# First heads and values split on VectorE, x ahead of the weights, gate operands ahead of the second norm, four banks in a turn

## The chip, the core and the metric

The kernel runs on one core of a Trainium2 chip. The metric is the device time of one execution in microseconds (us), the median of three runs. A core has five engines that each work through a queue of their own in order: TensorE (PE, matrix products), VectorE (DVE), ScalarE (ACT), GpSimd (POOL) and SyncE (SP), which here issues the transfers from the chip's memory (HBM) into SBUF. PE writes to PSUM, which has eight banks. An instruction that waits for another engine holds up what stands behind it in its own queue.

## The reference

Two layers of an encoder over 512 rows of width 1024. Layer 0 mixes rows with a gated linear recurrence (8 heads, both directions), layer 1 with latent attention (16 heads). Around both stand norms, a squared-ReLU MLP and a gated input per layer:

```python
for i in range(DEPTH):
    h = rms_norm(x, pre_mix[i])
    h = hgrn2_mixer(h, ...) if i == 0 else mla_mixer(h, positions, ...)
    x = x + rms_norm(h, post_mix[i])
    h = rms_norm(x, pre_mlp[i])
    h = jnp.square(jax.nn.relu(h @ w1[i])) @ w2[i]
    x = x + rms_norm(h, post_mlp[i])
    e = (p[i] @ w_ple_proj[i]) * jax.nn.sigmoid(x @ w_ple_gate[i])
    x = x + rms_norm(e, ple[i])
```

The mixers' inner loops are left out; no formula changes.

## The kernel before

**Tiling.** The 512 rows are four tiles of 128 rows. The first two tiles are called `a`, the last two `b`. Every product is made in three passes of split operands: an operand is rounded to a high part (`whi`, `ah`) and the remainder is the low part (`wlo`, `al`); PE then does high·high, low·high and high·low with 512 columns (256 where only one half of the rows is ready).

**Weights.** The class `Weights` (`W`) keeps a plan: transfers into buffers `raw` (two of them, `raw_bufs=2`), and pieces of 128x1024 called jobs. For each job ACT rounds `whi` (L109) and the job's engine subtracts to get `wlo`. That engine is `VN` (VectorE, written in a fixed order with its neighbours) unless the job names another one: `nc.vector` (VectorE, but free to be placed elsewhere in its queue) or `nc.gpsimd` (POOL; then in two halves, L112). `W.hold(keys)` splits up to four jobs ahead of what is used (`ahead=4`) and hands out the pieces; five pairs live at once (`split_bufs=5`). A `raw` buffer is free, and the next transfer is issued by SP, when the last job on it is split. Pieces are numbered in the plan's order.

**Queue order.** The program is written once; a scheduler sorts it into the queues. Where `keep(True)` is on, PE and `VN` instructions stay in the order of the source.

**The start.** `x0` to `x3` are loaded, tile 0 is normed (`normed((0,))`), then tile 1, then 2 and 3 together. The sum of squares is made by ACT for even tiles and by VectorE's `bn_stats` for odd ones; a chain of small VectorE instructions (`rq_i`, `rq_m`, `rq_n`, `rq_t`, `rx`) makes the reciprocal root. `first_values` multiplies with the four first value operands, numbers 0 to 3, which POOL splits. POOL also makes the rope tables.

**Mixer to MLP.** `mixer_to_mlp` multiplies the mixer's output with its gain row (`row("post_mix", l)`, loaded at the function's beginning, L837), adds the residual, norms, and turns.

**Turns.** `turned` turns a normed tile pair with PE (128x128 transposes against `ident`) into banks, from which ACT and VectorE split `ah` and `al`. There are three kinds of banks: `mm` (five), `sm` (two), `nm` (one). A turn uses four banks, one for each quarter of the width; with `sm` for all four the third quarter waits until the first has been read.

**MLP to gate.** In `mlp_to_gate` the last MLP products (`last`) of tiles `a` are made, then `chain(a)` norms them (`F` and `H`), `last` for `b`, `turned(a)`, `chain(b)`, then `W.hold` for the gate's operands 132 to 135, `gate` for `a`, `turned(b)`, `gate` for `b`. Layer 1 does the same with later numbers. Then comes the code that leads to the attention: `chain`, `turned` into the operands of `min` (145 and 146 are its last pieces).

**Attention's first part.** `query_latent`, `rope`, and per pair of heads `plan_heads`' three jobs (`uqn` 128x768, `uqr` 128x384, `ukv` 128x1024), all split by POOL; POOL also adds the rope terms (`rope_d`, L1291) and makes the remainders `stk` (L1367). The norms of the query and of the key/value latents are chains of small VectorE instructions (`nv`, `rq_...`, `nr`).

## Time and profile before

| | us |
|---|---|
| median of three runs | 1586.87 (1586.75 to 1590.89) |
| profiled execution | 1591.48 |
| its span on the core | 1589.8 |
| PE busy in it | 1529.7 (96 %) |
| VectorE, ACT, POOL busy | 1018.7, 772.3, 214.7 |

Three things are read from the trace: where PE stood idle and which engine ended that wait; in which stretches the granted clock of PE was half; and what the engine that ended the wait had been doing until then. In the rows, a bracket at the end gives the idle time just before an instruction and what released it; "x4" means four instructions in one row, whose time is that of the four together.

### The profile page before, as it was taken

To read this page: it belongs to the slowest core of one execution; us is meant where nothing else is said; L and a number is where in the kernel's file an instruction comes from. 1 tells how busy PE (TensorE), PEld (TensorE's weight loads), DVE (VectorE), ACT (ScalarE), POOL (GpSimd) and SP (SyncE) were. 2 spreads that over 40 slices of the span, in tenths; PEclk is the share of its full clock that TensorE was granted. 3 is DMA by queue.
4 is the path that set the end of the run, shared out by engine and by line. 5 is a ranking of instruction groups with operands and counts; after the bars stand their busy time and mean duration, and the time that the engine had idled before them with its cause. 6 is when DMAs were issued, how large, how long until landed. Compare 5 with 4: busy or idle time off the path is not lost.

```text
span 1589.8 us, 19297 instructions
## 1 busy us (share of the span) xinstructions
PE 1529.7 (96%) x7379; PEld 1265.5 (80%) x7379; DVE 1018.7 (64%) x1832; ACT 772.3 (49%) x1317; POOL 214.7 (14%) x232
## 2 busy tenths in 40 slices
PE   7999999998999999998898999999999999999987
PEld 6888888878888787876787888888788887878866
DVE  6678568653674949455757774378464748576365
ACT  4554455254654444433544654366355645454332
POOL 7133132200000000000125322342000000000000
PEclk8999999999999999999999999999999999999999
DMA  5622222145242322313411110211452140604211
GB/s 161 175 64 80 80 80 80 40 139 190 83 147 66 130 82 79 107 53 107 140 58 42 56 53 28 80 58 54 162 196 80 50 162 1 212 1 159 80 53 53
DMA packets 109951, 147.87 MB, mean 93 GB/s; under 512 B 4781, under 2 KB 78114, under 8 KB 109602
## 3 DMA queue, kind: packets, MB, share of 16 engines
q1 hardware_dynamic: 109282, 145.58, 28.1%
q8 instruction: 58, 0.95, 0.3%
q10 hardware_dynamic: 576, 1.05, 0.2%
q14 instruction: 35, 0.29, 0.1%
HBM read 138.23 MB, written 8.39 MB: 92 GB/s over the span
## 4 chain that ended last, share of the span: by engine, by line
PE 86%; DVE 8%; ACT 3%; issue 1%; DMA 1%; POOL 0%; SPq 0%; DVEq 0%; ACTq 0%; POOLq 0%
PE mm L147 80%; PE sm L147 5%; DVE wlo L147 1%; PE nm L147 1%; ACT whi L109 1%; DVE rq_t L147 1%; DMA x<-in_x 1%; DVE al L341 0%; DVE rope_d L1288 0%; DVE rope_d L1289 0%; DVE al L343 0%; DMA row<-in_gains 0%; ACT ah L342 0%; DVE ol L341 0%; ACT junk L855 0%
## 5 line engine op out<-in xcount | busy, mean ns | idle before, releaser
L147 PE MATMUL mm<-ah,whi 128*128 128x512 f32 (+1 forms) x912 | 333.9, 371 | 1.9 <-ACT e L996 0.9
L147 PE MATMUL mm<-ah,wlo 128*128 128x512 f32 (+1 forms) x912 | 330.9, 370 | 4.8 <-DVE wlo L147 4.8
L147 PE MATMUL mm<-al,whi 128*128 128x512 f32 (+1 forms) x912 | 319.2, 370 | 0.0
L109 ACT CAST whi<-raw 128x1024 fp32r<-128x1024 f32 (+3 forms) x195 | 196.8, 1016 | 251.8 <-PE mm L147 196.1
L147 DVE TENSOR_TENSOR wlo<-raw,whi 128x1024 fp32r<-128x1024 f32 x161 | 202.0, 1266 | 159.2 <-ACT whi L109 158.7
L147 PEld LDWEIGHTS mm<-ah,wlo 128*128 128x128 f32 x912 | 172.7, 189 | 32.5 <-DVE wlo L147 5.0
L147 PEld LDWEIGHTS mm<-ah,whi 128*128 128x128 f32 x912 | 172.7, 189 | 32.1 <-ACT whi L109 2.6
L147 PEld LDWEIGHTS mm<-al,whi 128*128 128x128 f32 x912 | 164.9, 190 | 28.2 <-DVE al L343 0.9
L147 PE MATMUL mm<-wlo,oh 128*128 128x512 f32 x400 | 159.3, 398 | 3.3 <-DVE wlo L147 3.3
L147 PE MATMUL mm<-whi,ol 128*128 128x512 f32 x400 | 157.7, 397 | 0.0
L147 PE MATMUL mm<-whi,oh 128*128 128x512 f32 x400 | 154.7, 400 | 2.8 <-DVE F L1039 2.8
L147 DVE TENSOR_TENSOR wlo<-r,whi 128x1024 fp32r<-128x1024 f32 x84 | 102.1, 1221 | 75.6 <-ACT whi L109 75.6
L109 ACT CAST whi<-r 128x1024 fp32r<-128x1024 f32 x84 | 87.1, 1049 | 86.9 <-PE mm L147 86.9
L147 PE MATMUL mm<-wlo,ah 128*128 128x512 f32 x304 | 120.5, 396 | 8.6 <-DVE wlo L147 8.6
L147 PE MATMUL mm<-whi,ah 128*128 128x512 f32 x304 | 120.7, 398 | 0.4 <-ACT ah L342 0.4
L147 PE MATMUL mm<-whi,al 128*128 128x512 f32 x304 | 119.8, 396 | 0.0
L147 PEld LDWEIGHTS mm<-wlo,oh 128*128 128x128 f32 x400 | 75.7, 189 | 22.7 <-DVE wlo L147 5.0
L147 PEld LDWEIGHTS mm<-whi,oh 128*128 128x128 f32 x400 | 75.6, 189 | 21.0 <-DVE F L1039 3.2
L147 PEld LDWEIGHTS mm<-whi,ol 128*128 128x128 f32 x400 | 75.7, 189 | 18.1
L147 PEld LDWEIGHTS mm<-wlo,ah 128*128 128x128 f32 x304 | 58.1, 191 | 21.4 <-DVE wlo L147 9.5
L340 ACT CAST oh<-Z 128x512 fp32r<-128x512 f32 x84 | 51.5, 620 | 46.2 <-PE mm L147 45.2
L112 POOL TENSOR_TENSOR wlo<-raw,whi 128x512 fp32r<-128x512 f32 (+2 forms) x60 | 59.1, 1014 | 108.8 <-ACT whi L109 78.3
(323 smaller groups left out, 2731.7 us busy)
## 6 DMA issues: line engine op xcount, KB each, us to landing
raw<-in_w_mlp_in SPq DMA_DIRECT2D x32, 1024.0 KB, 5.7
r<-in_w_mlp_out SPq DMA_DIRECT2D x24, 1024.0 KB, 9.6
raw<-in_hg_w_in SPq DMA_DIRECT2D x32, 512.0 KB, 4.8
raw<-in_w_mlp_out SPq DMA_DIRECT2D x8, 1024.0 KB, 5.1
raw<-in_w_ple_gate SPq DMA_DIRECT2D x8, 1024.0 KB, 5.4
raw<-in_mla_w_o SPq DMA_DIRECT2D x8, 1024.0 KB, 5.1
raw<-in_mla_w_uq SPq DMA_DIRECT2D x8, 576.0 KB, 4.0
raw<-in_hg_w_in SPq DMA_DIRECT2D x4, 1024.0 KB, 6.5
```

Of the source, the lines that this page charges most:

```text
L109: nc.scalar.copy(dst(hi), src(t))
L112: lo_eng.tensor_sub(dst(lo)[:, a], src(t)[:, a], f(dst(hi))[:, a])
L147: i = getattr(self.eng, name)(*args, **kw)
L340: A.copy(hi, src)
```

## The change

Six edits.
1. The four first value operands are split by `VN` (`None` means the default), not by POOL; the operands of head pairs 0 and 1 are split by `nc.vector`, not by POOL. The operands `w1(0, 2)` and `w1(0, 3)` of both layers are split by `nc.vector`, whose place in the queue is free, in place of `VN`.
2. Tile 1 of x is loaded ahead of the first weights, and its sum of squares is made by ACT.
3. The gain row of `post_mix` is loaded just after `H` in layer 0, at the start of the program, and before the call in layer 1.
4. `W.hold` for the gate's operands is called ahead of `turned(a)`, so ahead of `chain(b)`, with three pieces ahead in place of four.
5. The turns of `mlp_to_gate` and those to the attention take `sm, sm, mm, mm` (or `sm, sm, nm, mm`); the second turn of `mixer_to_mlp` takes `mm` in place of its second use of `sm`.
6. The rope addition of the key and of pair 0, and the `stk` remainders of pair 0, are VectorE's.

```diff
-                      G if half == 0 else nc.vector)
+                      None)
...
+            plan_pair([("w1", l, g, i), ("w1", l, g, i + 1)], w1[l], 0, c, c + P, nc.vector if (g, i) == (0, 2) else None)
...
     def plan_heads(pr):
+        eng = nc.vector if pr < 2 else G
...
-    W.prefetch(0)
     load(1)
     W.prefetch(1)
...
-            if t % 2 == 0:
+            if t < 3:
...
+    g_mix = [row("post_mix", 0, onp, 1)]
...
-        g1 = row("post_mix", l)
+        g1 = g_mix[l]
...
-        turned(b, an, (sm_tile, sm_tile, nm_bank, sm_tile))
+        turned(b, an, (sm_tile, sm_tile, nm_bank, mm_tile))
...
-        turned(a, (sm_tile,) * 4)
+        ws = W.hold([("pg", l, 0, q) for q in range(4)], 3)
+        turned(a, (sm_tile, sm_tile, mm_tile, mm_tile))
         chain(b)
         load_e(1)
-        ws = W.hold([("pg", l, 0, q) for q in range(4)])
...
-    turned(a, an, (sm_tile,) * 4)
+    turned(a, an, (sm_tile, sm_tile, mm_tile, mm_tile))
...
-    turned(b, an, (sm_tile,) * 4)
+    turned(b, an, (sm_tile, sm_tile, nm_bank, mm_tile))
...
-        G.tensor_add(dst, dst, a)
+        eng.tensor_add(dst, dst, a)
...
-                    G.tensor_sub(st[b], rt[a], f(st)[a])
+                    eng.tensor_sub(st[b], rt[a], f(st)[a])
```

Where the instructions move, at three places. At the start, SP's queue before: its first rows, in order.

```order
L478 DMA x0_9_87<-in_x 128x1024
L480 DMA graw_13_91<-in_gains 117x128
L81 DMA raw0_95<-in_hg_w_in 128x4x512
L478 DMA x1_10_88<-in_x 128x1024
L81 DMA raw1_98<-in_hg_w_in 128x4x512
```

And SP's first rows now.

```order
L480 DMA x0_9_87<-in_x 128x1024
L482 DMA graw_13_91<-in_gains 117x128
L480 DMA x1_10_88<-in_x 128x1024
L81 DMA raw0_96<-in_hg_w_in 128x4x512
L81 DMA raw1_98<-in_hg_w_in 128x4x512
```

The first weights, `raw0`, stand behind the second tile of x.

In `mlp_to_gate` of layer 0, VectorE's queue before, from the end of the second norm chain (`H` is the residual with the normed output added, two instructions; `wlo133` to `wlo135` are three of the gate's four low operands).

```order
L147 SCALAR_TENSOR_TENSOR rq_t_722_5882<-rq_t_722_5882 128x2
L147 SCALAR_TENSOR_TENSOR sr_503_3600<-rq_t_722_5882,sr_503_3600 128x2
L147 SCALAR_TENSOR_TENSOR rq_t_722_5882<-sr_503_3600,rq_n_721_5881 128x1 x2
L147 SCALAR_TENSOR_TENSOR sr_503_3600<-rq_t_722_5882,sr_503_3600 128x2
L147 SCALAR_TENSOR_TENSOR H_72_525<-F_427_2965,sr_503_3600,H_72_525 128x1024 x2
L147 TENSOR_TENSOR wlo133_5900<-raw52_5698,whi133_5899 128x1024
L147 TENSOR_TENSOR wlo134_5906<-raw53_5708,whi134_5905 128x1024
L147 TENSOR_TENSOR wlo135_5910<-raw53_5708,whi135_5909 128x1024
```

VectorE's queue now, from the `H` of the first norm chain on (`al0` is the first quarter of the turn of `a`).

```order
L147 SCALAR_TENSOR_TENSOR H_71_517<-F_427_2959,sr_502_3588,H_71_517 128x1024 x2
L1153 TENSOR_TENSOR F_427_2959<-F_427_2959,mm_710_5779 128x512
L147 TENSOR_TENSOR wlo133_5838<-raw52_5686,whi133_5837 128x1024
L1155 TENSOR_TENSOR F_427_2959<-F_427_2959,row_503_3589 128x512
L147 TENSOR_TENSOR wlo134_5844<-raw53_5696,whi134_5843 128x1024
L1153 TENSOR_TENSOR F_427_2959<-F_427_2959,mm_712_5808 128x512
L147 TENSOR_TENSOR wlo135_5848<-raw53_5696,whi135_5847 128x1024
L343 TENSOR_TENSOR al0_682_5547<-sm_714_5853,ah0_681_5546 128x2x256
L343 TENSOR_TENSOR al1_684_5549<-sm_715_5860,ah1_683_5548 128x2x256
```

The three splits moved from behind the second chain to ahead of the turn's first `al`.

In attention's first part, VectorE's queue before (`nacc` sums the squares for a norm, `cql` is a low part of the query latent).

```order
L147 TENSOR_TENSOR wlo146_6692<-raw59_6288,whi146_6691 128x1024
L424 TENSOR_TENSOR nacc_805_6688<-nacc_805_6688,nsq_809_6742 128x512
L343 SCALAR_TENSOR_TENSOR cql0_820_6778<-mm_791_6424,gains_4_78,cqh0_819_6777 128x512
L424 TENSOR_TENSOR nacc_802_6685<-nacc_802_6685,nsq_821_6781 128x512
L1288 TENSOR_TENSOR rope_d_825_6818<-mm_808_6716,SIN_798_6663 32x512
```

The same stretch of VectorE's queue now, with the operands of pair 0 in it.

```order
L147 TENSOR_TENSOR wlo146_6680<-raw59_6276,whi146_6679 128x1024
L112 TENSOR_TENSOR wlo147_6686<-raw60_6287,whi147_6685 128x768
L426 TENSOR_TENSOR nacc_804_6676<-nacc_804_6676,nsq_808_6727 128x512
L112 TENSOR_TENSOR wlo148_6690<-raw60_6287,whi148_6689 128x384
L345 SCALAR_TENSOR_TENSOR cql0_819_6763<-mm_790_6412,gains_4_78,cqh0_818_6762 128x512
L426 TENSOR_TENSOR nacc_801_6673<-nacc_801_6673,nsq_820_6766 128x512
L345 SCALAR_TENSOR_TENSOR cql1_822_6770<-mm_791_6413,gains_4_78,cqh1_821_6769 128x512
L112 TENSOR_TENSOR wlo149_6696<-raw61_6683,whi149_6695 128x1024
L1288 TENSOR_TENSOR rope_d_824_6802<-mm_807_6701,SIN_797_6651 32x512
```

The three low operands of pair 0 now stand on VectorE between the pieces of the two norms; 150 to 152, those of pair 1, follow further down the same queue.

## Rows read from the trace of the kernel before

**Rows 1.** The page: busy time, share of the span and instructions of each engine.

```profile
PE 1529.7 (96%) x7379; PEld 1265.5 (80%) x7379; DVE 1018.7 (64%) x1832; ACT 772.3 (49%) x1317; POOL 214.7 (14%) x232
```

**Rows 2.** Waits of PE: line, releaser; us in total, times, longest.

```profile
PE mm L147 <- DVE wlo L147: 16.7, 7, 4.8
PE sm L147 <- DVE al L341: 5.5, 6, 1.1
...
PE mm L147 <- DVE x L522: 2.4, 2, 2.1
```

**Rows 3.** Stretches: length, busy us of each engine, granted clock, DMA share, GB/s.

```profile
14.28:27.94 13.66, 10.84 (x29) 8.41 (x30) 13.41 (x38) 5.64 (x12) 12.55 (x20) 0.50 0.61 165
...
369.27:372.68 3.41, 3.41 (x19) 3.41 (x18) 1.13 (x4) 0.70 (x1) 0.00 (x0) 0.50 0.72 211
720.84:727.67 6.83, 4.46 (x11) 3.50 (x12) 4.59 (x4) 0.00 (x0) 0.00 (x0) 0.50 0.44 159
...
812.00:870.00 58.00, 51.52 (x256) 41.65 (x256) 46.35 (x95) 31.46 (x57) 31.26 (x29) 0.97 0.23 68
```

**Rows 4.** Timeline of the start: time, duration, engine, line, operation, idle before.

```profile
9.80 1.99 ACT L109 CAST whi<-raw 128x1024 fp32r<-128x1024 f32 x2 [2.26 <-DMA raw<-in_hg_w_in]
...
11.11 1.29 DVE L516 BATCH_NORM_STATS2 bn_st<-x 128x6 f32<-128x512 f32 x2 [1.99 <-DMA x<-in_x]
...
17.21 1.21 DVE L147 SCALAR_TENSOR_TENSOR rq_t<-rq_t 128x1 f32<-128x1 f32 x1
...
20.90 0.16 DVE L147 SCALAR_TENSOR_TENSOR rx<-rq_t,rx 128x1 f32<-128x1 f32 x1
...
10.93 9.92 POOL L112 TENSOR_TENSOR wlo<-raw,whi 128x512 fp32r<-128x512 f32 x8 [7.87 <-ACT whi L109]
```

**Rows 5.** Timeline at the mixer's output: PE, ACT, VectorE.

```profile
330.94 0.50 PE L147 MATMUL mm<-whi,oh 128*128 128x512 f32 x1 [2.79 <-DVE F L1039]
...
327.32 0.60 ACT L855 ACTIVATE junk<-mm 128x512 f32<-128x512 f32 x1 [4.34 <-PE mm L147]
...
330.19 1.29 DVE L1039 TENSOR_TENSOR F<-mm,row 128x512 f32<-128x512 f32 x2 [6.49 <-DMA row<-in_gains]
```

**Rows 6.** Timeline at the first MLP operands: PE, ACT, VectorE.

```profile
368.93 0.39 PE L147 MATMUL mm<-ah,wlo 128*128 128x256 f32 x1 [4.76 <-DVE wlo L147]
...
358.27 1.04 ACT L109 CAST whi<-raw 128x1024 fp32r<-128x1024 f32 x1
...
361.55 2.48 DVE L147 SCALAR_TENSOR_TENSOR H<-F,sr,H 128x1024 f32<-128x1024 f32 x2
```

**Rows 7.** Timeline from the MLP to the gate, layer 0: PE, VectorE.

```profile
723.21 0.80 PE L147 MATMUL mm<-wlo,ah 128*128 128x512 f32 x1 [4.32 <-DVE wlo L147]
723.80 0.63 PE L147 MATMUL mm<-whi,al 128*128 128x512 f32 x1
724.23 0.63 PE L147 MATMUL mm<-whi,ah 128*128 128x512 f32 x1
...
729.29 0.40 PE L147 MATMUL mm<-whi,ah 128*128 128x512 f32 x1
729.52 0.39 PE L147 MATMUL mm<-wlo,ah 128*128 128x512 f32 x1
...
719.54 2.48 DVE L147 SCALAR_TENSOR_TENSOR H<-F,sr,H 128x1024 f32<-128x1024 f32 x2
721.94 3.49 DVE L147 TENSOR_TENSOR wlo<-raw,whi 128x1024 fp32r<-128x1024 f32 x3
```

**Rows 8.** Timeline of the turn to the attention: PE.

```profile
780.03 1.94 PE L147 MATMUL sm<-ident,r 128*128 128x128 f32 x8 [3.00 <-DVE rq_m L147]
...
786.35 0.28 PE L147 MATMUL mm<-ah,whi 128*128 128x256 f32 x1
```

**Rows 9.** Timeline of the attention's first part: PE.

```profile
827.44 0.65 PE L147 MATMUL nm<-ident,nr 128*128 128x128 f32 x4 [1.44 <-DVE nr L147]
...
849.17 0.50 PE L147 MATMUL mm<-Kh,Qh 128*128 128x512 f32 x1 [1.85 <-ACT P L1384]
```

More of the change, by code (lines that the diff above doesn't have):

```diff
@@ L119, in prefetch, with hold @@
         self._load(i)
-    def hold(self, keys):
-        self._split(self.n_used + self.ahead)
+    def hold(self, keys, ahead=None):
+        self._split(self.n_used + (self.ahead if ahead is None else ahead))
         return [self._take(key) for key in keys]
@@ L232, in w1_plan @@
             c = g * 1024 + i * P
-            plan_pair([("w1", l, g, i), ("w1", l, g, i + 1)], w1[l], 0, c, c + P)
+            plan_pair([("w1", l, g, i), ("w1", l, g, i + 1)], w1[l], 0, c, c + P, nc.vector if (g, i) == (0, 2) else None)
     def plan_rows(key, src, r0, g, lo=None):
@@ L305, in plan_heads @@
         W.job(("uqn", pr), r, [(lambda t: t[:, :768].rearrange("p (k h n) -> p k h n", h=2, n=P),
-                                     lambda t: hv(t)[:, :, :, :P])], lo=G)
+                                     lambda t: hv(t)[:, :, :, :P])], lo=eng)
         W.job(("uqr", pr), r, [(lambda t: t[:, :384].rearrange("p (k h n) -> p k h n", h=2, n=64),
-                                     lambda t: hv(t)[:, :, :, P:])], lo=G)
+                                     lambda t: hv(t)[:, :, :, P:])], lo=eng)
         r = W.raw([(lambda t: cols(t, 2, 512),
                           w_ukv[:, pr * 512 : pr * 512 + 512].rearrange("(k p) n -> p k n", p=P))])
-        W.job(("ukv", pr), r, [(lambda t: t[:, :1024], lambda t: t[:, :1024])], lo=G)
+        W.job(("ukv", pr), r, [(lambda t: t[:, :1024], lambda t: t[:, :1024])], lo=eng)
     for pr in range(5):
@@ L592, in trunk @@
     tables("natural_log_exp_and_others")
+    zp = rowp = r2 = None
     h_cm = right("h0")
@@ L600, in trunk, with row @@
     onp = on_cm.__enter__()
+    def row(name, l, pool=None, bufs=2):
+        t = T(pool or rowp, [P, D], "row", bufs)
+        r = ROW[name] + l * NB
+        nc.sync.dma_start(t, all_gains[r : r + NB, :].rearrange("(o a) b -> o (a b)", o=1).to_broadcast([P, D]))
+        return t
+    g_mix = [row("post_mix", 0, onp, 1)]
     ons = []
@@ L831, in trunk @@
     espill = nc.dram_tensor("e_spill", (2, NT, P, D), F32).ap()
-    def row(name, l):
-        t = T(rowp, [P, D], "row", 2)
-        r = ROW[name] + l * NB
-        nc.sync.dma_start(t, all_gains[r : r + NB, :].rearrange("(o a) b -> o (a b)", o=1).to_broadcast([P, D]))
-        return t
     def guess(v, y):
@@ L1183, in mlp_to_gate @@
             last(t, 1, ws)
-        turned(a, (sm_tile,) * 4)
+        ws = W.hold([("pg", l, 0, q) for q in range(4)], 3)
+        turned(a, (sm_tile, sm_tile, mm_tile, mm_tile))
         chain(b)
         load_e(1)
-        ws = W.hold([("pg", l, 0, q) for q in range(4)])
         for t in a:
             gate(t, 0, ws)
-        turned(b, (sm_tile,) * 4)
+        turned(b, (sm_tile, sm_tile, mm_tile, mm_tile))
         for t in b:
@@ L1206, in close_mlp @@
             c.__exit__(None, None, None)
-    zp = rowp = r2 = None
     rows_k(n0, range(NT), ons, 7, w)
-    row_cm = right("row0")
-    rowp = row_cm.__enter__()
     act, pss, eps = mixer_to_mlp(0, 0, ons, n0)
-    row_cm.__exit__(None, None, None)
     on_cm.__exit__(None, None, None)
@@ L1282, in trunk, with rope @@
     nkv.rs(FULL)
-    def rope(ps, dst):
+    def rope(ps, dst, eng=G):
         a = T(mp, [P, S], "rope_a", 1)
@@ L1313, in trunk @@
         ckv.append((hi, lo))
-    rope(pss[5], kr)
+    rope(pss[5], kr, V)
     krh, krl = T(mp, [P, S], "krh", dt=F32R), T(mp, [P, S], "krl", dt=F32R)
@@ L1361, in project_q @@
                 rt = T(mp, [P, S], "rope_d", 2)
-                rope(ps, rt)
+                eng = G if pr else V
+                rope(ps, rt, eng)
                 for jj in range(2):
@@ L1440, in trunk @@
     row_cm = right("row1")
-    rowp = row_cm.__enter__()
+    g_mix.append(row("post_mix", 1, row_cm.__enter__(), 1))
     act, pss, eps = mixer_to_mlp(1, 1, xs, n0)
```

## Prediction

> **What bounds the kernel now.** I read the page first: PE is busy 1529.7 us of the span of 1589.8 [rows 1], and the change leaves PE's products as they are. So the time is a stream of matmuls plus the holes in it, and an edit is worth what it takes out of the holes. Second, PE's waits by releaser: the largest group is low operands that VectorE had not yet split, 16.7 us in seven waits, the longest 4.8; the second kind are waits inside turns, 5.5 us in six [rows 2]. Third, the granted clock by stretch: behind the longer holes PE runs at half rate (0.50, the level of 1.2 GHz) for 3.4 us or 6.8 us, and at the start for 13.66 [rows 3]. At half rate a 512-column matmul follows the one before it after 0.43 us (723.80 to 724.23), at full rate after 0.23 (729.29 to 729.52) [rows 7], so of each busy us in such a stretch 1 - 0.23/0.43 = 0.465 us is lost: 3.41 busy cost 1.6, the 4.46 busy behind the gate's hole cost 2.1, the 10.84 busy at the start cost 5.0 [rows 3]. A hole thus has two prices. Last, the timelines around each hole: who ended it and what that engine did until then.
>
> **The change part by part.** The sum is made against the profiled execution, 1591.48 us; it lies 4.61 above the median of the timed runs, 1586.87, and I give the result against the median.
>
> *Mixer's gain row, layer 0.* PE waits 2.79 us for `F` on VectorE, which itself waits for the row's transfer until 330.19; the sum of squares that `F` also needs begins at 327.32 and takes 0.60 [rows 5]. With the row loaded at the start, `F` (two in 1.29) can end by about 328.6, and PE, back at 330.94 before, by about 328.7: 2.2 saved. A hole of 0.6 is left; the half-rate stretch behind it (3.4 us, as in [rows 3]) should go: 1.6. Together 3.8.
>
> *First MLP operands.* PE waits 4.76 us for a `wlo` whose `whi` was ready at 358.27 + 1.04 = 359.3; between them in VectorE's fixed order stand the norm chain and `H`, 2.48 us from 361.55 [rows 6]. Placed freely, this `wlo` goes ahead of `H`, before PE asks at 364.2. All 4.76 goes and the half-rate stretch behind it, 3.41 busy: 1.6. What is late next is `H`, moved back by one split (3.49/3 = 1.16 us [rows 7]), and with it the second half's turn; PE reaches that turn some 11 us after the hole, so the delay is covered. If that cover were gone it would cost up to 1.2. The turn's fourth quarter gets its own bank: 0.9, in both layers. Together 7.3 for layer 0 and 0.9 for layer 1, which had no such hole.
>
> *Gate operands, both layers.* In layer 0 PE waits 4.32 us, until 723.21, because three `wlo` (3.49 us from 721.94) stand behind the second chain's `H` (2.48 us from 719.54) [rows 7]. Now they stand ahead of the first `al` of the turn, where VectorE waits for ACT and PE anyway. The hole goes, and with it 2.1 of half rate. The two turns hold about 2.7 us of holes here (1.6 in the first, 1.1 in the second, three of the six in [rows 2]); with four banks the second's goes, while the first keeps about 0.8, since its first `al` now stands behind the third `wlo`, which can't start before ACT has cast it. Saved: 4.3 + 2.1 + 1.1 + 0.8 = 8.3. New on VectorE's queue: the second chain stands behind three splits and ends at about 723.4 rather than 722.0. PE needs it only after 48 matmuls of the gate, 48 x 0.23 = 11 us from about 716, at 727. That covers it. The next `raw` is free some 10 us earlier, as the splits are, so SP issues it earlier too and ACT's next cast waits less. Layer 1 repeats the pattern with a stretch of 3.4 us: 4.3 + 1.6 + 1.1 + 0.8 = 7.8.
>
> *Turn to the attention.* PE waits 3.00 us inside the first turn, until 780.03, and is back on the `min` products at 786.35 [rows 8]. With two more banks the transposes go through by about 778, the filler products by 781; then the accumulators want the same banks, and the wait for their splits moves there, until about 782.6. I take 3.7 off and give back 0.8, half the price of a half-rate stretch that may stay. The second turn saves 1.2 by its banks, but PE now arrives about 4 us earlier than its operand allows for: 0.8 back. Together 3.3, bounds 1 and 6.
>
> *The start.* Before, ACT casts `raw0` from 9.80, x1 has landed by 11.11, and POOL's eight halves take 9.92 us from 10.93. In that time four `rq_t` steps of the tile-1 norm need 1.2 each (one of them at 17.21) where the same kind takes 0.16 at 20.90, after POOL [rows 4]. So x1 was scaled 4 us late. By the order `raw0` now lands between 9.8 (as before) and about 11.1, when both transfers were in before. I take 10.8, nearer to the second: minus 1.0. Two splits of 1.2 stand ahead of the first `al`: minus 0.5. PE's wait for the scaled tile 1, the longest of 2.1 us [rows 2], goes. The half-rate stretch should shorten from 13.66 to 6.8; with 6.8 busy it costs 3.2 in place of 5.0. I expect a little more from the steps that no longer wait, 0.6. Together 3.2, bounds -1 and 6. On SP's queue `H` and the row now stand ahead of the fifth weight buffer and wait for ACT's table; that buffer's pieces are fifth in line for PE, four pieces' products of some 5 us each before them, which hide it; uncovered it would cost the few us of `H`'s transfer.
>
> The Trainium skill, "DMA: Bandwidth & Descriptors", section "Queues, rings and completion order", speaks against this edit: a copy is spread over rings whose descriptors are consumed in order. By that rule `raw0` would come at the upper bound, 11.1, and the sum would be 0.3 smaller.
>
> *Attention's first part.* VectorE takes six operands, 2 x (768 + 384 + 1024 columns) at 1.16 per 1024 = 4.9 us, two rope additions and two `stk` subtractions, 0.7 each as an estimate from `F`'s 1.29 for two of the same width [rows 5], 2.8: 7.7 us. It was busy 46.35 of 58 us there, POOL 31.26 [rows 3]. Against it stands the stretching of small steps while POOL runs, as at the start (1.21 where 0.16 is usual [rows 4]); over the two chains here I estimate it at 7 us, seven steps of that kind. The totals nearly cancel; the order doesn't. I walked VectorE's queue with unstretched times: the norm's result `nr`, for which PE waited 1.44 before [rows 9], comes 1.2 later, behind four low operands; the later chain, which ends PE's wait of 1.85 at 849.17 [rows 9], is 3 us later. So I charge 3.0. Bounds: 7.7 if nothing of the stretching goes away, and a gain of 4 if nearly all holes of this part (5 us) go.
>
> The Trainium skill, "SBUF — State Buffer", section "SBUF: two separate sides", says that VectorE and POOL share a port pair that one of them holds for a whole instruction while the other blocks. The `rq_t` at 17.21 took 1.21, as long as one POOL half, 9.92/8 = 1.24 [rows 4], so the trace agrees. By it alone, without the order, this part would lose 0.7 rather than 3.0, and the time would be 1553.
>
> **Sum:** 3.8 + 7.3 + 0.9 + 8.3 + 7.8 + 3.3 + 3.2 - 3.0 = 31.6. From the profiled execution that gives 1559.9, from the median 1555.3. I say 1555.3.
>
> **The rivals.** First, the attention's first part gains by 3 where I charge 3, since stretching was the whole cause of its waits: 1549. For it speaks the equal length of steps and POOL halves, against it that the splits stand ahead of the chain. Second, VectorE becomes the bound there: 7.7 lost in place of 3.0 and two more half-rate stretches (3.2): 1555.3 + 4.7 + 3.2 = 1563. For it speaks 46.35 of 58 us. Third, the gate's holes close only in part: the first `al` of the turn waits behind `wlo` 133 to 135 so long (3.49 in a row) that a hole of 3 and a half-rate stretch stay in each layer, 2 x (2.2 + 1.6) = 7.6: 1563. Against it: in that place VectorE waits for ACT and PE, and the splits fill those waits.
>
> Fourth, slower than before: PE's clock stays at half rate through the whole attention start. If VectorE's queue keeps a hole open every few us from 812 to 870, the 51.52 busy us there [rows 3] would cost 0.465/0.535 = 0.87 us more each, 45 us, and with 4.7 for the queue the time is 1555 + 50 = 1605. It decides from the point where holes of two us come back as often as the stretches behind them are long; before, the mean clock there was 0.97 [rows 3], with one hole of that size. It needs all of it to undo 31.6.
>
> That an operand is not moved as said is ruled out by the order shown above.
>
> **How the numbers follow.** The forecast has 0.60, the first rival 0.13, the second 0.12, the third 0.10, the fourth 0.02; 0.03 is left for what I don't see. About 0.3 % (4.8 us) is what a measurement here can tell from no change. All but the fourth and a part of the rest lie below 1582: faster 0.95, same 0.025, slower 0.025. The bounds of the start, the turn and the attention's part, added in quadrature about the forecast, are some 8 us either side. The range 1546 to 1568 takes in this and the first three rivals.
>
> **What would show it.** In the profile after: no wait of PE on `wlo` above 1 us; `F` at the mixer's output released by ACT, not by a transfer; the gate's stretch at clock 1.0; POOL idle in the attention's first part and small VectorE steps at 0.16 there; the hole before the `nr` transposes grown to about 2.2. Wrong would be: new holes of 2 us or more at the turns, a `raw` that lands later and stops ACT, or half-rate stretches where I see none.

## The result: 1587.9 to 1549.7 us

| | before | after |
|---|---|---|
| median | 1587.93 us (1586.75 to 1590.89) | 1549.74 us (1549.0 to 1550.72) |
| profiled execution, its span | 1591.48, 1589.8 | 1550.72, 1549.0 |

The ratio is 0.9757, 95 % interval 0.974 to 0.9774: 38.2 us faster by the medians of four runs each. The prediction was 1555.3, range 1546 to 1568, faster with a chance of 0.95. The time lies in the range, 5.6 below the forecast. That small miss is made of several larger ones, and one term had the wrong sign when it was tried alone.

To see where the time came from, take the n-th matmul of PE's queue in both traces and subtract the start times (a few neighbours swap places, which costs no accuracy over a stretch). At 700.03 of the trace before this lead is 15.28 us, at 745.08 it is 24.94: the gate of layer 0 gave 9.66. By stretch:

| stretch, in times of before | predicted | measured |
|---|---|---|
| start, to 46.6 | +3.2 | +2.92 |
| last head of the mixer, 286 to 300 | 0 | +1.38 |
| mixer's gain row, 300 to 350 | +3.8 | +3.66 |
| first MLP operands and turn, 350 to 390 | +7.3 | +7.80 |
| 390 to 500 | 0 | -0.43 |
| gate of layer 0, 700 to 745 | +8.3 | +9.66 |
| turn to the attention, 770 to 812 | +3.3 | +6.35 |
| attention's first part, 812 to 870 | -3.0 | -0.06 |
| MLP turn of layer 1, 1175 to 1200 | +0.9 | +1.28 |
| 1200 to 1400 | 0 | -0.43 |
| gate of layer 1, 1510 to 1555 | +7.8 | +9.09 |
| sum | 31.6 | 41.2 |

The sum of the two traces is 3.0 above the 38.2 of the medians. The profiled execution of before lies 3.55 above its median, that of after 0.98 above its, and 0.4 is lost behind the last matmul. Held against the forecast's 31.6, the stretches gave 9.6 more.

### The profile page after: what moved, and what is told of

The parts are those of the page before. It is cut to its first block, busy times and chain, and to the rows that moved or that the text cites. A ratio compares the mean times of both kernels' runs of the same rounds, so it can differ in the third digit from the quotient of the medians.

```text
span 1549.0 us, 19274 instructions
## 1 busy us (share of the span) xinstructions
PE 1513.7 (98%) x7379; PEld 1254.9 (81%) x7379; DVE 1016.5 (66%) x1842; ACT 771.8 (50%) x1319; POOL 189.2 (12%) x208
## 4 chain that ended last, share of the span: by engine, by line
PE 89%; DVE 6%; ACT 3%; issue 1%; DMA 1%; POOL 0%; SPq 0%; DVEq 0%; ACTq 0%; POOLq 0%
PE mm L147 83%; PE sm L147 5%; PE nm L147 1%; DVE wlo L147 1%; ACT whi L109 1%; DMA raw<-in_hg_w_in 1%; ACT ah L344 0%; ACT junk L859 0%; DVE rq_t L147 0%; DVE rope_d L1288 0%; DVE rope_d L1289 0%; DVE ol L343 0%; DVE r L265 0%; DVE F L892 0%; DVE mx L1382 0%
## 5 line engine op out<-in xcount | busy, mean ns | idle before, releaser
L147 DVE TENSOR_TENSOR wlo<-raw,whi 128x1024 fp32r<-128x1024 f32 x165 | 207.5, 1267 | 151.0 <-ACT whi L109 150.8
L112 POOL TENSOR_TENSOR wlo<-raw,whi 128x512 fp32r<-128x512 f32 (+2 forms) x40 | 38.1, 977 | 566.6 <-ACT whi L109 559.6
L147 PE MATMUL mm<-whi,r 128*128 128x512 f32 x208 | 68.4, 396 | 0.0
```

The costliest lines, as they stand in the source:

```text
L112: lo_eng.tensor_sub(dst(lo)[:, a], src(t)[:, a], f(dst(hi))[:, a])
L147: i = getattr(self.eng, name)(*args, **kw)
```

## The profile after

The page of the changed kernel, busy time and share of the span; it answers to [rows 1]. PE is busy 16.0 less with the same number of matmuls; fewer of them run at half rate.

```profile
PE 1513.7 (98%) x7379; PEld 1254.9 (81%) x7379; DVE 1016.5 (66%) x1842; ACT 771.8 (50%) x1319; POOL 189.2 (12%) x208
```

The waits of PE in the changed kernel: line, releaser, us in total, times, longest. It answers to [rows 2]: `wlo` fell from 16.7 to 3.3, and the waits of `sm` on `al` from 5.5 to a single one of 0.2. The first row is the scaled x at the start: its longest wait, 2.6, is a new one, for tile 0.

```profile
PE mm L147 <- DVE x L523: 3.4, 2, 2.6
PE mm L147 <- DVE wlo L147: 3.3, 4, 0.8
PE mm L147 <- ACT P L1385: 2.4, 2, 2.0
...
PE mm L147 <- DVE al L343: 0.6, 2, 0.3
PE mm L147 <- DVE rq_m L147: 0.5, 1, 0.5
```

Stretches of the changed kernel: length, busy us of PE, PEld (PE's loading of weights), VectorE, ACT, POOL, granted clock, DMA share, GB/s. The first is the half-rate stretch at the start (13.66 long in [rows 3]), the second the last head of the mixer, the third the gate of layer 0, the fourth the turn to the attention, the fifth the attention's first part from the same matmul to the same matmul as 812.06 to 870.04 before, the sixth its half-rate stretch.

```profile
12.16:22.90 10.74, 9.70 (x24) 6.18 (x25) 9.74 (x20) 7.04 (x17) 6.29 (x11) 0.53 0.92 255
283.23:295.76 12.53, 10.50 (x63) 8.82 (x62) 9.38 (x31) 4.68 (x15) 2.36 (x4) 1.00 0.12 47
701.28:715.16 13.88, 13.88 (x71) 11.57 (x69) 11.53 (x27) 6.87 (x13) 0.00 (x0) 1.00 0.33 113
751.96:770.38 18.42, 17.38 (x133) 16.37 (x132) 13.39 (x39) 11.23 (x24) 4.89 (x12) 1.00 0.65 233
780.80:838.84 58.04, 52.50 (x257) 42.33 (x255) 47.84 (x105) 30.84 (x57) 13.92 (x14) 0.97 0.22 67
818.01:821.42 3.41, 3.41 (x9) 2.67 (x10) 2.24 (x8) 3.11 (x9) 0.24 (x1) 0.54 0.00 0
```

And the same stretch of the attention in the kernel before:

```profile
812.06:870.04 57.98, 51.50 (x257) 41.63 (x255) 46.35 (x95) 31.50 (x57) 31.27 (x30) 0.97 0.23 68
```

Timeline of the changed kernel (time, duration, engine, line, operation, idle before). The mixer's `F` is now released by ACT, not by the row's transfer, and PE waits 0.64 where it waited 2.79 [rows 5]. At the gate the third `wlo` ends just ahead of the first `al`, the second chain's `H` comes behind them at 705.08 instead of ahead, and PE waits 0.30 where it waited 4.32 [rows 7]. In the turn to the attention the 3.00 of [rows 8] is gone; the 0.71 ahead of it stood there before as well (until 776.04), and 0.55 is new. The last row is the wait that is now the longest behind the start; `P` are the softmax's exponentials, `r` is the normed tile.

```profile
323.80 1.41 DVE L1043 TENSOR_TENSOR F<-mm,row 128x512 f32<-128x512 f32 x2 [4.33 <-ACT junk L859]
324.55 0.50 PE L147 MATMUL mm<-whi,oh 128*128 128x512 f32 x1 [0.64 <-DVE F L1043]
...
698.85 1.22 DVE L147 TENSOR_TENSOR wlo<-raw,whi 128x1024 fp32r<-128x1024 f32 x1
699.99 1.28 DVE L343 TENSOR_TENSOR al<-sm,ah 128x512 fp32r<-128x512 f32 x2
700.73 0.50 PE L147 MATMUL mm<-whi,al 128*128 128x512 f32 x1 [0.30 <-DVE al L343]
705.08 2.48 DVE L147 SCALAR_TENSOR_TENSOR H<-F,sr,H 128x1024 f32<-128x1024 f32 x2
...
751.13 0.98 PE L147 MATMUL sm<-ident,r 128*128 128x128 f32 x7 [0.71 <-ACT r L1230]
756.56 0.36 PE L147 MATMUL mm<-ah,whi 128*128 128x256 f32 x1 [0.55 <-DVE rq_m L147]
...
818.01 0.56 PE L147 MATMUL mm<-Kh,Qh 128*128 128x512 f32 x1 [2.05 <-ACT P L1385]
```

## The experiments

Each edit below is made on the changed kernel unless it says otherwise. Where one kernel holds two edits, they lie 310 us or more apart, and each is read in its own stretch by the lead over the kernel before. The intervals of the medians are about 0.15 % either side, some 2.3 us; the leads by stretch repeat much closer wherever the half-rate stretches are the same (the gate of layer 0 gave 9.60 to 9.66 in ten traces that hold its two edits).

### The same kernel again

> The changed kernel once more, for comparison with the two below on the same chip: 1549.7 within 2; its start, which was 2.92 shorter than before in the first profile and 2.97 to 5.10 in four others with the same start, again between 2.5 and 5.5.

The median is 1549.89 (1548.27 to 1550.67). The lead at the start was 4.93 this time, against 2.92, and in the last head of the mixer -0.02, against +1.38: the stretch of the same matmuls, which had clock 1.00 above, has 0.88 here, as before had.

```profile
281.18:295.12 13.94, 11.91 (x64) 10.43 (x63) 9.38 (x31) 4.69 (x15) 2.29 (x4) 0.88 0.10 38
5.70:41.67 35.97, 30.02 (x143) 23.06 (x142) 25.01 (x83) 22.56 (x47) 17.14 (x38) 0.95 0.51 163
```

So the 1.38 that nothing in the sum explains isn't the change's. In all fourteen traces of this study PE waits 1.6 there for the same `state`; in four of them a half-rate stretch follows, in ten none does. The second row is the start, from the same matmul to the same matmul as 6.04 to 46.60 before. Its idle time (length less PE's busy time), 5.95, is longer than the 4.74 of the first profile below, but its clock is better, 0.95 against 0.86:

```profile
6.02:43.69 37.67, 32.93 (x144) 25.02 (x142) 26.70 (x83) 23.12 (x47) 17.19 (x38) 0.86 0.55 177
```

### All turns with the banks of before

```diff
-turned(a, (sm_tile, sm_tile, mm_tile, mm_tile))
+turned(a, (sm_tile,) * 4)          # likewise the other turns of edit 5
```

> The changed kernel with the banks of all turns as they were before (sm four times; sm, sm, nm, sm in the mixer's second turn). By the forecast the banks alone are worth: 0.9 in each mixer-to-MLP turn, 1.1 in each gate's second turn and 0.8 in the first, 3.3 in the turn to the attention: 0.9 x 2 + 1.9 x 2 + 3.3 = 8.9, so 1558.6. The turn to the attention measured 6.35 in place of 3.3; theory 1: the banks are worth all of it, then 1561.6, its hole of about 3 and the half-rate stretch of 6.8 us behind it come back; theory 2: half of it came from the gate, whose operands and results are earlier now, then the hole at the turn stays below 1.5 and no half-rate stretch follows: about 1556.

The median is 1563.14, the ratio to the kernel before 0.983 (0.9816 to 0.9843). The gates fell from 9.66 and 9.09 to 6.66 and 6.23, so the banks are worth 3.0 and 2.9 there, not 1.9. The MLP turns lost 1.29 and 1.27, and the -0.43 behind each of them went to 0.00 and -0.03, so this small loss is a part of that edit. The turn to the attention fell from 6.35 to 1.11: theory 1, all but a sixth is the banks'. The half-rate stretch behind its hole is back too, 3.41 long where the kernel before had 6.82. PE's waits in its timeline:

```profile
701.05 1.25 PE L147 MATMUL sm<-ident,H 128*128 128x128 f32 x8 [1.64 <-DVE al L343]
715.31 1.25 PE L147 MATMUL sm<-ident,H 128*128 128x128 f32 x8 [1.14 <-DVE al L343]
...
758.16 1.75 PE L147 MATMUL sm<-ident,r 128*128 128x128 f32 x8 [2.74 <-DVE sv L147]
```

The third is the hole of 3.00 in [rows 8]: earlier gate results shorten it by only 0.26.

### The gate's operands late, and the first values on POOL

```diff
-        ws = W.hold([("pg", l, 0, q) for q in range(4)], 3)      # ahead of turned(a)
+        ws = W.hold([("pg", l, 0, q) for q in range(4)])         # behind chain(b), load_e(1)
...
-                      None)                                     # first values: VN
+                      G if half == 0 else nc.vector)
```

> The changed kernel with two edits undone that lie 680 us apart and are read each in its own stretch. First, the gate's operands are held after the second chain again (four pieces ahead), the four banks stay. Forecast: the hole of 4.3 and the half-rate stretch behind it (2.1 in layer 0, 1.6 in layer 1) come back: 6.4 and 5.9 lost. Rival: the hole is longer than before, since the four banks let PE arrive earlier at the missing operand; then 7.5 and 7. Second, the four first value operands are split by POOL again. Forecast's theory: POOL stretches the steps of tile 1's norm to 1.2 each, x1 is scaled several us later, the start loses 2 to 3. Rival: x1 lands ahead of the weights now, its norm ends before POOL begins, the start stays within 1. Sum: 1564.5 by the forecast, 1562 to 1565 by the rivals.

The median is 1566.16, the ratio 0.9852 (0.9838 to 0.9867). The gates fell to 1.34 and 1.03: 8.3 and 8.1 lost, beyond even the rival, which expected a longer hole. (The edit also brings back four pieces ahead in place of three; what that part does alone wasn't tried.) VectorE and PE of this kernel:

```profile
701.60 2.48 DVE L147 SCALAR_TENSOR_TENSOR H<-F,sr,H 128x1024 f32<-128x1024 f32 x2
704.00 3.49 DVE L147 TENSOR_TENSOR wlo<-raw,whi 128x1024 fp32r<-128x1024 f32 x3
705.27 0.80 PE L147 MATMUL mm<-wlo,ah 128*128 128x512 f32 x1 [6.42 <-DVE wlo L147]
```

With four banks PE is through the turn 2.0 earlier and then waits 6.42 for the same `wlo` rather than 4.32. So each of the two edits hides behind the other: without the hold the banks give 1.34, without the banks the hold gives 6.66, together they give 9.66.

At the start the result contradicts the forecast. The lead is 5.59 with POOL, and 2.92 to 5.10 with VectorE. Tile 1's chain is over when x1 is scaled at 11.66, before POOL's first piece, so POOL no longer stretches it; and PE's waits for the scaled tile 1 (0.75 in the changed kernel), for an `ah` (0.67) and for an `al` (0.24) are gone. VectorE, POOL, and the stretch of the start as above:

```profile
11.66 0.75 DVE L523 TENSOR_SCALAR x<-x,rx 128x1024 f32<-128x1024 f32 x1
...
11.96 10.30 POOL L112 TENSOR_TENSOR wlo<-raw,whi 128x512 fp32r<-128x512 f32 x8 [8.89 <-ACT whi L109]
...
5.87:41.01 35.14, 31.83 (x142) 25.01 (x142) 23.60 (x79) 19.50 (x42) 26.33 (x41) 0.90 0.57 177
```

Idle time is 3.31 here, against 4.74 and 5.95 in the two profiles of the changed kernel and 3.78 to 5.95 in all seven traces with its start.

### w1(0, 2) and w1(0, 3) in the fixed order, and the weights first

```diff
-            plan_pair([...], w1[l], 0, c, c + P, nc.vector if (g, i) == (0, 2) else None)
+            plan_pair([...], w1[l], 0, c, c + P, None)
...
+    W.prefetch(0)
     load(1)
```

> The changed kernel with two edits undone that lie 350 us apart. First, the operands w1(0, 2) and w1(0, 3) are in VectorE's fixed order again. Forecast: PE's wait of 4.76 at the first MLP operands and its half-rate stretch (1.6) come back, 6.4 lost in layer 0, nothing in layer 1. Rival: the fourth bank of the turn already shortened what stands ahead of that operand, then 3 to 5 lost. Second, the first weights are loaded ahead of tile 1 of x again. Forecast's theory: raw0 lands 0.5 earlier (9.8), x1 lands later, and the start changes by under 1. Rival: x1's late landing alone made the long half-rate start, then 2 to 3 lost. Sum: 1556 by the forecast, 1558.5 by the second rival.

The median is 1557.46, the ratio 0.98 (0.9786 to 0.9815). The first MLP operands fell from 7.80 to 1.28: 6.52 lost, forecast 6.4, and the old wait is back to the hundredth:

```profile
362.14 0.44 PE L147 MATMUL mm<-ah,wlo 128*128 128x256 f32 x1 [4.76 <-DVE wlo L147]
...
13.45 0.50 PE L147 MATMUL nm<-whi,ah 128*128 128x512 f32 x1 [3.82 <-ACT ah L344]
22.93 1.06 PE L147 MATMUL mm<-ident,x 128*128 128x128 f32 x8 [1.95 <-DVE ss L521]
...
21.76 1.03 DVE L524 TENSOR_SCALAR x<-x,rx 128x1024 f32<-128x1024 f32 x1
```

The start's lead was 1.78, against 2.92 to 5.10 with tile 1 first: 1.1 to 3.3 lost, nearer to the second theory. The second and third rows show it: `raw0` is cast at 10.11, little earlier than otherwise, but ACT's sum of the late x1 stands ahead of its `ah`, and tile 1 itself is awaited for 1.95. The last row bears on what made x1 late in the kernel before. POOL splits nothing here, and the steps of tile 1's chain take 0.15 to 0.37, yet x1 is scaled at 21.76, no earlier than the 21.10 of before: VectorE's own splits and `al` now stand between the steps.

### The gain row late, and tile 1's sum on VectorE

```diff
-    g_mix = [row("post_mix", 0, onp, 1)]
+    g_mix = []                # row("post_mix", 0, ...) just ahead of mixer_to_mlp
...
-            if t < 3:
+            if t % 2 == 0:
```

> The changed kernel with two edits undone that lie 310 us apart. First, the gain row at the mixer's output is loaded late again. Forecast: 2.2 of the wait for F and the half-rate stretch (1.6) come back, 3.8 lost. Rival: the half-rate stretch doesn't come back, as it doesn't follow every hole of two us: 2.2 lost. Second, the sum of squares of tile 1 is made by VectorE's bn_stats again. Forecast's theory: nothing at the start depends on it. Rival, from the trace of the changed kernel: there the norm chain of tile 0 stood still from 7.3 to 8.8 behind a step that waits for ACT's sum of tile 1; with bn_stats this stop goes and x0 is scaled about 1.5 earlier, the first product comes 0.5 to 1.2 earlier. Sum: 1553.5 by the forecast, 1552.5 by the rival at the start.

The median is 1560.71, the ratio 0.9821 (0.9805 to 0.9838); that is 7 to 8 slower than the two sums. The gain row behaved: the lead in its stretch fell from 3.66 to 0.54, so 3.1 lost; the wait was 2.34 and a half-rate stretch followed. The rest went at the start, whose lead was -3.36, 6.3 to 8.5 less than with the changed kernel's. VectorE, ACT and PE there:

```profile
7.52 1.29 DVE L517 BATCH_NORM_STATS2 bn_st<-x 128x6 f32<-128x512 f32 x2 [0.90 <-DMA x<-in_x]
...
10.18 0.75 DVE L523 TENSOR_SCALAR x<-x,rx 128x1024 f32<-128x1024 f32 x1
...
36.00 0.31 ACT L588 ACTIVATE sin_t<-ang 128x128 f32<-128x128 f32 x1 [2.60 <-POOL ang L584]
...
37.46 0.79 PE L147 MATMUL mm<-whi,ah 128*128 128x512 f32 x1 [4.50 <-ACT ah L344]
...
332.52 0.80 PE L147 MATMUL mm<-whi,oh 128*128 128x512 f32 x1 [2.34 <-DVE F L1043]
```

Neither theory saw this. My rival expected tile 0's chain to be free of its stop; it waits for x1 just the same, now behind `bn_stats`, and x0 is scaled at 10.18. And the change of one instruction moved another one far away: the sine of the rope table now stands in ACT's queue ahead of six of the eight `ah` of tiles 2 and 3, and waits there for POOL. PE waits 4.50 for it. This hole is a matter of the queue's order, not of the engine that makes the sum.

### The heads' work back on POOL: all, the splits, the rope

```diff
-        eng = nc.vector if pr < 2 else G       # splits of pairs 0 and 1
+        eng = G
...
-    rope(pss[5], kr, V)                        # rope additions, remainders
+    rope(pss[5], kr)
...
-                eng = G if pr else V
+                eng = G
```

> The changed kernel (1549.7 us), with the operands of head pairs 0 and 1, the rope additions of the key and of pair 0, and the remainders of pair 0 given back to POOL; all else as changed. Theory of the forecast (the order of VectorE's queue costs 3.0 in the attention's first part): 1549.7 - 3.0 = about 1546.7, and the last wait on P below 2.05. Rival (small VectorE steps are stretched while POOL runs, and that alone made the holes): the nr chain grows again, a hole of about 1.4 comes back ahead of the nr transposes, perhaps with a half-rate stretch of 3.4 us (1.6): 1551 to 1553. Third (neither, the part is set by the last chain in both): within 0.6 of 1549.7, the last wait on P between 1.8 and 2.1.

> The changed kernel, only the low operands of head pairs 0 and 1 given back to POOL (4.9 us of VectorE work by the forecast); rope additions and remainders stay on VectorE. Forecast's theory: the nr chain comes 1.2 earlier, but PE's wait there is gone already, so 0 to 1.2 gained. Rival (stretching): the small steps of the nr chain are long again (1.2 in place of 0.16) and the wait for nr of about 1.4 is back: 1551 to 1552.5.

> The changed kernel, only the three rope additions and remainders (kr, pair 0; 2.8 us of VectorE work by the forecast) given back to POOL; the splits stay on VectorE. Forecast's theory: VectorE's last chain, on which PE waits 2.05 for P, ends up to 1.8 earlier: 1548 to 1549. Rival (stretching): the chain's last steps stand beside POOL's additions and become longer, the wait on P grows by 0.5 to 1.5: 1550 to 1552. If neither, the wait stays at 2.0 within 0.3.

With all on POOL the median is 1547.99 (1547.57 to 1548.28), the ratio 0.9736 (0.9723 to 0.975); with only the splits 1550.72 and 0.9753 (0.974 to 0.9767); with only the rope 1549.62 and 0.9746 (0.9733 to 0.976). The leads gained in the attention's first part are +1.62, -1.66 and +0.38, against -0.06. First its stretch with all on POOL:

```profile
779.71:836.07 56.36, 52.65 (x256) 42.41 (x255) 45.90 (x95) 30.72 (x57) 31.00 (x30) 0.97 0.23 70
```

With the splits alone on POOL:

```profile
778.62:838.26 59.64, 53.80 (x256) 43.21 (x255) 45.91 (x99) 30.74 (x57) 25.54 (x26) 0.94 0.22 66
...
816.40 0.80 PE L147 MATMUL mm<-Kh,Qh 128*128 128x512 f32 x1 [3.27 <-ACT P L1385]
```

And with the rope alone:

```profile
780.16:837.76 57.60, 52.46 (x257) 42.35 (x255) 48.23 (x101) 30.78 (x57) 20.05 (x18) 0.97 0.22 68
...
818.45 0.50 PE L147 MATMUL mm<-Kh,Qh 128*128 128x512 f32 x1 [0.53 <-ACT P L1385]
```

The direction was the forecast's: the work is worth 1.7 less on VectorE than on POOL here, against 3.0 charged. But the parts don't add up: by the leads the splits back on POOL are a loss of 1.6, the rope a gain of 0.4, both together a gain of 1.7. Most of the loss of 1.6 is the clock's. Behind its hole half rate lasts 6.83, where the changed kernel has 3.41, and idle time is 5.84 against 5.54. `gate_late_values_pool`, whose code in this stretch is the changed kernel's, has -1.46 there, with half rate twice:

```profile
786.41:845.84 59.43, 54.05 (x257) 43.57 (x255) 47.84 (x105) 30.82 (x57) 13.89 (x14) 0.94 0.22 66
```

So I go by idle time, which holds little of the clock (5.38 in that kernel): 5.84 with the splits alone on POOL, 5.14 with the rope alone, 3.71 with both, against 5.54. The gain of both, 1.8, stands; the loss of the splits alone isn't shown. In VectorE's queue the place of the query norm's last step, `nrq`, differs, which `P` needs: with the splits alone on POOL five row maxima `mx` stand ahead of it, it comes at 815.08, and PE waits 3.27 for `P`. That this is why the parts don't add up is read from the trace, no edit here tests it. (That kernel loses another 1.15 up to 1000, which I didn't follow up.)

The steps beside POOL are indeed stretched, with all on POOL (the step of 0.16 falls between the two `stk`):

```profile
810.88 0.92 DVE L147 TENSOR_TENSOR rq_t<-rq_t,rq_m 128x4 f32<-128x4 f32 x1
811.84 0.16 DVE L147 SCALAR_TENSOR_TENSOR rq_t<-rq_t 128x4 f32<-128x4 f32 x1
812.04 1.13 DVE L147 SCALAR_TENSOR_TENSOR nr<-rq_t,nr 128x4 f32<-128x4 f32 x1
...
810.51 2.63 POOL L1368 TENSOR_TENSOR stk<-rope_d,stk 64x512 fp32r<-64x512 f32 x2
```

Still this kernel is the faster one in this stretch. The stretching is real and was not what set the time.

### The query's norm early

```diff
+    with tc.high_priority():          # beside the edit of heads_pool
         nq.rs(FULL)
         ...                           # rq, nrq
```

> The kernel in which POOL has the heads' work again (1548.0, with waits of 0.92, 0.71 and 0.54 and 2.9 us at half rate in the attention's first part), and in addition the small steps of the query's norm are placed as early in VectorE's queue as their inputs allow. If the place of these steps in the queue sets the wait on P, the wait of 0.54 goes and with it perhaps the half-rate stretch: 0.5 to 2 gained, 1546 to 1547.5. If what is left are waits for banks that the rope's five reads hold, and for Kl behind them, nothing is gained: 1548 within 0.5.

The median is 1547.27, the ratio 0.9733 (0.9718 to 0.9747). The lead gained in the attention's first part is 2.79, and 2.82 twice in the two kernels below that hold the same edit; the half-rate stretch is gone:

```profile
780.72:835.91 55.19, 51.53 (x257) 41.06 (x256) 45.15 (x95) 30.71 (x57) 30.82 (x29) 1.00 0.24 71
...
816.62 0.50 PE L147 MATMUL mm<-Kh,Qh 128*128 128x512 f32 x1 [1.00 <-ACT P L1386]
```

The wait on `P` didn't go, it grew from 0.54 to 1.00, while two others shrank; idle time is 3.66 against 3.71. So the 1.2 are the half-rate stretch. Whether its absence follows from the order or from chance isn't shown: all three traces with this edit are without it, but there is only one of `heads_pool` to hold against them.

### The heads on VectorE, alone, in the kernel before

Made on the kernel before:

```diff
     def plan_heads(pr):
+        eng = nc.vector if pr < 2 else G       # lo=eng in its three jobs
...
-    rope(pss[5], kr)
+    rope(pss[5], kr, V)
...
+                eng = G if pr else V           # rope and stk of pair 0
```

> The kernel before with one edit alone: the operands of head pairs 0 and 1, the rope additions of the key and of pair 0 and the remainders of pair 0 are VectorE's. Forecast's theory: this edit by itself costs 3.0 in the attention's first part (the wait for nr 1.2 longer, the last chain 1.8 later). By its price inside the changed kernel (1.7, from giving it back to POOL): 1.7 slower. Rival (the steps beside POOL were stretched, nothing else): the wait for nr of 1.44 goes, 1.4 or more faster. All of it inside 0.3 % of the whole, so it is read from the shift of the same PE instructions in that part.

The median of ten runs is 1586.67, the ratio 0.998 (0.9971 to 0.999): 0.2 % faster, clear of no change. The lead in the attention's first part is +2.51, the opposite of the 3.0 I charged.

```profile
807.38:862.85 55.47, 50.60 (x257) 41.88 (x255) 46.67 (x106) 32.35 (x59) 11.72 (x14) 0.97 0.22 71
...
832.70 1.22 PE L147 MATMUL mm<-ckh,whi 128*128 128x512 f32 x2 [4.73 <-ACT ckh L341]
```

Idle time is 4.87 against 6.48. The waits for `nr`, for `Kl` and on `P` are gone, and one of 4.73 took their place, for `ckh`, a high part of the key/value latent: the `nr` transposes stand behind all `cqh` products in PE's queue (827.37), and the `P` from which `ckh` is cast then stands on VectorE behind four `rope_d` (to 831.25). `two_banks` has the same wait of 4.73 at the same products, and its lead in this stretch is -0.22: half rate lasts 6.82 behind the wait instead of 3.41, some 1.1 of the difference, and two later waits of 0.73 and 0.53 are there that this trace doesn't have. The same edit, then, gains 2.5 in one program and loses 1.7 in the other; by idle time it gains 1.6 and loses 1.8.

### Towards a better kernel

```diff
 heads_pool_query_early, and in addition
-                      None)                   # first values
+                      G if half == 0 else nc.vector)
```

> The changed kernel with the first values split by POOL again, the heads' work on POOL again, and the query's norm steps early in VectorE's queue. By the stretches measured one by one: the attention's first part +2.8 in place of -0.1, the start +5.6 in place of 2.9 to 5.1: 1549.7 - 2.9 - 1.5 = 1545.5. If POOL's splits at the start gave nothing and the 5.6 was one good case of the clock: 1547.

The median is 1545.66 (1544.55 to 1546.35), the ratio 0.9728 (0.9713 to 0.9742); the start's lead was 6.11, the second case with POOL above all seven with VectorE. It is 4.2 below the changed kernel on the same chip, 1549.89, and the runs of the two don't overlap.

```diff
 pool_values_heads_query, and in addition
+    VN.keep(True)
+    scaled((0,))        # sum, chain and scaling of tile 0, then of tile 1,
+    scaled((1,))        # in VectorE's fixed order, ahead of the turns
...
+    VN.keep(False)
...
+    VN.tensor_add(tot, es[0], es[1])    # a small sum, fixed behind them
```

> The same with the norms of tiles 0 and 1 whole and in this order in VectorE's queue, so that tile 0 isn't stopped behind the step that waits for ACT's sum of tile 1. If this stop (x0 scaled at 9.4 rather than about 7.9) sets the first product: 0.5 to 1 more gained, 1544.5 to 1545. If the first product waits for the cast of raw0 (landing at 10.3 to 10.8), nothing: as the kernel above.

The median is 1543.91 (1543.56 to 1546.11), the ratio 0.972 (0.9706 to 0.9735). x0 is scaled at 7.46 instead of 9.40, but the first product starts at 12.47 instead of 12.58, since the cast of `raw0` begins at 10.16 and 10.27: the lead at the start is 6.03 against 6.11, and the medians, 1.75 apart, overlap in their runs. The early norm is hidden by the weights' landing. Both are faster than the changed kernel.

## Why the prediction was right, and where it was wrong

**Right: the holes that VectorE's fixed order made.** The first MLP operands (+7.3 forecast, 7.8 measured; 6.52 by undoing the operand's edit, 1.29 by the banks) and the mixer's row (3.8 and 3.66; 3.1 by undoing it) came as worked out from [rows 5, 6], hole and half-rate stretch each. What was late next, `H`, did no harm.

**Mis-sized: the gates, 8.3 and 7.8 against 9.66 and 9.09.** The hole with its stretch gave 6.7 in layer 0 (6.4 in the sum), the first turn 1.46 (0.8), the second 1.5 (1.1). I left 0.8 in the first turn for an `al` behind three `wlo`; it was 0.30. The sum also priced banks and hold as if they were independent; undone one by one they cost 3.0 and 8.3, more than both are worth.

**Mis-sized: the turn to the attention, 3.3 against 6.35.** I let the accumulators wait until 782.6 for the same splits, and gave back 0.8 for half rate in the first turn and 0.8 for a late operand in the second. PE begins these products at 756.56, which by the lead of 24.91 at the stretch's start is 781.47 in times of before, after a wait of only 0.55, and clock 1.00 holds through the turn: 4.92 to the `min` products, where I had 2.9. In the second turn PE does wait, 0.50, and still gains 1.43, where I had 0.4. The step that failed is "the wait moves there": the splits don't keep their old times. The last of the first turn's eight `al` in the changed kernel, and in the kernel before:

```profile
756.54 0.47 DVE L345 SCALAR_TENSOR_TENSOR al<-mm,gains,ah 128x256 fp32r<-128x256 f32 x1
...
786.92 0.47 DVE L343 SCALAR_TENSOR_TENSOR al<-sm,gains,ah 128x256 fp32r<-128x256 f32 x1
```

In times of before the first ends at 781.92, 5.5 earlier than the second. With four banks all eight stand ahead of the next chain's `H`; with two, before and in `two_banks`, `H` stands ahead of the last of them.

**Wrong: the attention's first part, -3.0 against -0.06.** The walk of VectorE's queue put `nr` 1.2 late. It isn't late: it is done 15.3 after the stretch's first matmul in both kernels, and in the changed trace PE finds it ready. I had walked the queue of the new program against PE's order of the old one, while the order of both changed, with the transposes of `nr` behind others. Alone, in the kernel before, the edit gains 2.51; in the changed kernel it costs 1.7. The near zero is the sum of that cost and of a gain of 1.6 that the same stretch has without it. Idle time fell from 6.48 to 3.71 between the kernel before and `heads_pool`: the wait of 1.44 for `nr` is gone and that of 1.85 on `P` is 0.54, while PE's busy time grew by 1.15. What moved these waits stays open. Nor is POOL idle in the changed kernel, as I had said: 13.92 busy, 31.27 before.

The Trainium skill, "SBUF — State Buffer", section "SBUF: two separate sides", has VectorE, where an instruction reads two inputs from SBUF, and POOL take turns at a shared port pair, the other one blocked for a whole instruction. The rows above agree for the single step (0.92 and 1.13 beside POOL, 0.16 else). By this rule alone giving the work back to POOL should have cost time; it gained 1.7, so the rule doesn't settle on which engine the work belongs.

**Right in sum, wrong in its parts: the start, 3.2 against 2.92.** The number can't be held against one profile: seven traces with the same start code gave 2.92, 2.97, 3.44, 3.58, 4.06, 4.93 and 5.10, and two with the start of before differ by 2.22. The terms I gave for it add up to 3.0, not 3.2. In its parts, tile 1 ahead of the weights is a gain of 1 to 3, and the splits on VectorE are a loss of some 2 (3.9 on average, 5.59 and 6.11 with POOL). PE's wait for the scaled tile 1 didn't go but fell from 2.09 to 0.75, and one of 2.60 for tile 0 came, whose chain now stops for ACT's sum of tile 1. The half-rate stretch, 6.8 in the forecast, was 10.24 in the first profile and 3.41 in the second. I had blamed POOL's stretching for the late x1, but `w1_fixed_weights_first` has x1 as late with the splits on VectorE. Once x1 lands early its chain is over before POOL begins, and the remedy for that is not needed any more.

The Trainium skill, "DMA: Bandwidth & Descriptors", section "Queues, rings and completion order", by which each ring takes its descriptors in order, had spoken for the bound of 11.1 for `raw0`. It wasn't reached: the cast began between 9.99 and 10.83 in the eleven traces with tile 1 first, 10.3 on average, against 9.01, 9.80 and 10.11 in the three with the weights first. The weights do land later, by some 0.7 where I took 1.0.

**The rivals.** The first rival's time, 1549, is the measured one by luck, not by its mechanism: the attention's first part didn't gain 3. The second (VectorE the bound there, 7.7 lost) didn't come, nor did the third (a hole of 3 left at the gates) and the fourth (half rate all through the attention's start): -0.06, and clock 1.00 and 0.97 in the rows above.

## What to carry to other kernels

Two edits at one place share one hole: price them together, and undo them one at a time, before trusting either number. Work that was moved because of a collision should be tried back when another edit has moved the collision; here both groups moved to VectorE, the first values and the heads, were better on POOL once the rest was in place. Where a scheduler writes the queues, an edit's price holds for one program only: look at the order around it again, on every engine that takes part, also where the edit isn't. And before a stretch's gain or loss is laid to an edit, split it into idle time and clock: here the same code lost 1.4 by the clock alone.

## What the hardware showed

A hole's second price, the half-rate stretch, is not fixed: the same wait of 1.6 at the mixer's last head was followed by half rate in four of fourteen traces, at a cost of 1.4. Identical starts differ by 2.2 us in their lead, mostly for the same reason: over the same matmuls the granted clock was 0.95 in three of the seven, with leads of 4.06 to 5.10, and 0.86 in four, with leads of 2.92 to 3.58. What decides it these runs don't show. A single trace can thus tell holes to a tenth of a us, but the clock behind them only to some two us in each such place.
